# Signed branch outputs and adding DMAs for the right operand of two projection phases

## The chip, the cores and the metric

The kernel runs on one core of a Trainium2 chip. The metric is the device time of one execution in microseconds (us), shown as the median of several runs. The core has a matrix engine (PE), a vector engine (DVE), an activation engine (ACT), a general engine (POOL, GpSimd) and a queue engine (SP). They run beside each other and meet at semaphores. DMA transfers are issued from the queues of SP, ACT and POOL and are carried by sixteen DMA engines. In this kernel only transfers issued on POOL's queue add to what lies at their target; those of SP and ACT copy.

## The reference

The reference is one layer of an encoder: a stream of 1024 positions of width 1024 (16 learned meta tokens stand ahead of it inside), a retention branch and a windowed attention branch, and a merge of both.

```python
u = _rms_norm(h, pre_w)
z = u @ w_in
rq, rk, rv, rg, aq, ak, av, ag, gr, ga = _split_in(z)
...                                              # o_r: retention, normed per head; o_a: attention
o_r = o_r * ret_nw * silu(rg);   y_r = o_r @ w_rb
o_a = o_a * silu(ag);            y_a = o_a @ w_ab
mix = sigmoid(gr) * y_r + sigmoid(ga) * y_a
return h + _rms_norm(mix @ w_o, post_w)
```

All is float32. The change concerns the operands of `o_r @ w_rb` and `o_a @ w_ab`: two products of 1024 by 1024 matrices.

## The kernel before, in words

**Precision.** A float32 product is made of three matmuls of rounded parts: high times high, low times high, high times low (`mm3`, lines 74 to 79). So every operand is split first: ACT writes the rounded high part (a copy with a cast), DVE the low part, which is the source less the high part (`dve_lo`, line 92).

**Order of the work.** First come the projections for retention with retention itself (to about 330 us), then attention with its projections (to about 555 us), and then four phases that are run by one routine (`run`, line 1191): z (the gates, sixteen units of 256 output channels), r (the product with w_rb, four units), a (the product with w_ab, four units) and o (the output projection). Retention writes its transposed, normed and weighted result to the DRAM tensor `oTr_d` (`finish`, lines 591 to 604: two transposes on PE, two ACT copies with the scale of one column of `rnw`, a DMA per two chunks). Attention writes to `oTa_d` (`stage3`, line 1487: an ACT copy out of PSUM). In phase z the first eight units multiply these two tensors in place by the SiLU of their gates (`z_post`, line 1236).

**The four phases.** Each product is made by the Winograd form of Strassen's scheme: seven block products in place of eight. The left operand is the weights, in blocks A11 to A22 of a unit (128 channels by 512). The right operand is the stream in four blocks of 512 by 512, B11 to B22; the first index is the half of the contraction, the second the half of the positions. The table `PROD` (line 929) names the products:

```python
PROD = {1: ("A11", "B11"), 2: ("A12", "B21"), 3: ("S4", "B22"), 4: ("A22", "T4"), 5: ("S1", "T1"),
        6: ("S2", "T2"), 7: ("S3", "T3")}
```

Here S1 = A21 + A22, S2 = S1 - A11, S3 = A11 - A21, S4 = A12 - S2, and T1 = B12 - B11, T2 = B22 - T1, T3 = B22 - B12, T4 = B21 - T2. The S are made by DVE in `Phase.prepare` (line 978) and split by `Phase.split` (line 972), which is called up to LEAD = 6 products ahead of its use. `Phase.product` (line 1019) issues a product's 12 `mm3` matmuls, and `Phase.combine` (line 1055) empties PSUM: ACT copies some accumulators, DVE adds others, and the `post` routine of the phase follows. Per pair of units the order of products is 1, 5, 6, 2, 7, 3, 4, each for both units in turn.

**The right operand of the next phase** is made while the last fourteen products of a phase run. `refill` (line 1141) gives a table of hooks, counted back from the end of the phase: `load` brings a block in four tiles of 128 by 512 from DRAM (on SP's queue, `act_src`, line 1221), `t1`, `t2`, `t3` and `b21` subtract tiles on DVE (`minus`, line 1152), and `plain` or `split_b` (line 948) splits a tile into its place, where the phase before has read its operand for the last time. There is one refill in phase z (the operand of r, out of `oTr_d`, tiles named z) and one in phase r (the operand of a, out of `oTa_d`, tiles named r). The refill in phase a, for the output weights, has another path: its T blocks were computed earlier and are loaded. The tiles of blocks (0,0) and (1,0) come from a pool with seven places, those of (0,1) and (1,1) from one with eight; a load waits until a place is free.

**What sets the order.** The program is written in the order of the products and hooks. A planner (the tile framework) then simulates the program with its own costs and fixes each engine's order of instructions, taking what is ready in its simulation with the earliest place in the program. On the chip each engine works its list strictly in order: an instruction that waits holds up all behind it on that engine. In retention and attention many places are pinned by hand (`follow`, `issue_after`); in the four phases few are.

**POOL** has no compute in the four phases but one power per row of the output. Its queue carries adding DMAs in phase a (`y_post`, line 1287, into `mx_d`) and in phase o (`o_out`, line 1345, into the output).

The names in the profile follow the tiles: bz, br, ba and bo are the PSUM banks of the phases; lhz, llz, lhr, llr and so on the high and low parts of the left operand; big and T the places of the right operand (T2 to T4 share the name T).

Of the kernel before, what the change touches and what calls it, by code (L numbers as in the profile page):

```python
# [7 lines left out]
F32 = mybir.dt.float32  # L8
R = mybir.dt.float32r
AF = mybir.ActivationFunctionType  # L10
ALU = mybir.AluOpType
# [5 lines left out]
P = 128  # L17
KT = D // P
# [15 lines left out]

def cols(c):
    return (0, NM) if c == 0 else (NM + P * (c - 1), NM + P * c)


@with_exitstack
def block_kernel(ctx: ExitStack, tc: tile.TileContext, x0, xT, x, meta, w_in, w_rb, w_ab, w_out, post_w,  # L40
                 rope, tab, out):
    nc = tc.nc
    PSUM = bass.MemoryType.PSUM

    keep = ctx.enter_context(tc.tile_pool(name="keep", bufs=1))
# [45 lines left out]
    def dve_lo(o, i, hi):  # L91
        return nc.vector.tensor_tensor(o, i, hi.bitcast(F32), ALU.subtract).ins  # L92


    vec = keep.tile([P, 2 * KT], F32, name="vec")
# [1 line left out]
    dtab = keep.tile([P, 28], F32, name="dtab")  # L97
    rcol = keep.tile([P, 9], F32, name="rcol")
    rbc = keep.tile([P, T], F32, name="rbc")
    rnw = keep.tile([P, KT], F32, name="rnw")  # L100
    mhalf = keep.tile([P, 40], F32, name="mhalf")
    nc.vector.memset(mhalf, -0.5)

    def fetch_w(src, u):
# [161 lines left out]
    with tc.tile_pool(name="setup", bufs=1, reuse_waits="tile") as st:  # L266
# [61 lines left out]
        for k in range(KT):  # L328
            t = xr[k]
# [19 lines left out]
        decay_columns()  # L349
        with follow(low):  # L350
            nc.vector.tensor_scalar(nsink, head[:, 29:37], -1.0, None, op0=ALU.mult)
            nc.vector.tensor_copy(rnw, vec[:, KT:2 * KT])
            done = pack_meta()
        split, wv0 = halves_w(U_V)
        raw = fetch_w(w_in, U_V)
# [4 lines left out]
        for c in range(9):  # L360
            a, b = cols(c)
            t = st.tile([P, D if c < 7 else T], F32, tag="xn" if c < 7 else "xr", bufs=7 if c < 7 else KT - 1,
                        name=f"xn{c}")[:, 0:D]
# [94 lines left out]
    def retention(h, fill, begin=lambda: None):  # L458
# [132 lines left out]
        def finish(c):  # L591
            o = op[c - 1]
            to = p1(f"to{h}_{c}")
            for e_ in range(2):
                latest[:] = [nc.tensor.transpose(to[:, P * e_:P * e_ + P], o[:, P * e_:P * e_ + P], ident).ins]
            if c % 2 == 0:
                ost[0] = rp.tile([P, 2, 256], F32, tag="ost", bufs=2, name=f"ost{h}_{c}")
            w0 = P * ((c - 1) % 2)
            for e_ in range(2):
                nc.scalar.activation(ost[0][:, e_, w0:w0 + P], to[:, P * e_:P * e_ + P], AF.Copy,  # L600
                                     scale=rnw[:, 2 * h + e_:2 * h + e_ + 1])
            if c % 2 == 1:
                nc.sync.dma_start(
                    oTr_d[2 * h:2 * h + 2, :, P * (c - 1):P * (c + 1)].rearrange("e p t -> p e t"), ost[0])
# [343 lines left out]
    def split_b(n, k, src):  # L948
        (h, as_), (l, _) = (right(n, s, k) for s in range(2))
        nc.scalar.copy(h, as_(src))  # L950
        dve_lo(l, as_(src), h)

    class Phase:
        def __init__(self, nm, seq, load, post, fetch=None, apart=(), early=(), pre={}):
            self.nm, self.load, self.post, self.fetch, self.pre = nm, load, post, fetch, pre
            self.seq = [(u, p) for u, p in seq if p not in pre.get(u, ())]
            self.apart, self.early = apart, early
            self.raw, self.s, self.ops, self.u, self.e = {}, {}, {}, {}, {}
            self.cur = None

# [10 lines left out]

        def split(self, u, p, src):
            h, l = (lp.tile([P, 4, P], R, tag=t, bufs=LEAD, name=f"{t}{self.nm}{u}_{p}") for t in ("lh", "ll"))
            nc.scalar.copy(h, src)  # L974
            dve_lo(l, src, h)
            self.ops[u, p] = h, l

        def prepare(self, u, p):
            if self.cur is not None and u // 2 != self.cur:
                self.raw = {}  # L980
            self.cur = u // 2
            g = nc.vector.tensor_tensor
            made = {1: 2, 6: 3}.get(p)
            if made not in self.pre.get(u, ()):
                made = None
            for q in (p, made):
                if self.fetch and q in POST and u not in self.early:
                    self.fetch(u, *POST[q])
            if made:
                self.e[u, made] = gtile(f"e{u}{made}")  # L990
                nc.sync.dma_start(self.e[u, made], e_d[u, made])
            if p in (1, 2, 4):
                self.split(u, p, self.block(u, PROD[p][0]))
            elif p == 7:
                t = lp.tile([P, 4, P], F32, tag="st", bufs=3, name=f"st{self.nm}{u}S3")
                g(t, self.block(u, "A11"), self.block(u, "A21"), sub)
                self.split(u, 7, t)
            elif p == 5:
                t = self.s[u] = lp.tile([P, 4, P], F32, tag="st", bufs=3, name=f"st{self.nm}{u}S")
                g(t, self.block(u, "A21"), self.block(u, "A22"), add)  # L1000
                self.split(u, 5, t)
                g(t, t, self.block(u, "A11"), sub)
            elif p == 6:
                t = self.s[u]
                self.split(u, 6, t)
                if u in self.early or 3 in self.pre.get(u, ()):
                    del self.s[u]
                else:
                    g(t, self.block(u, "A12"), t, sub)
            elif u in self.early:  # L1010
                t = lp.tile([P, 4, P], F32, tag="st", bufs=3, name=f"st{self.nm}{u}S4")
                g(t, self.block(u, "A21"), self.block(u, "A22"), add)
                g(t, t, self.block(u, "A11"), sub)
                g(t, self.block(u, "A12"), t, sub)
                self.split(u, 3, t)
            else:
                self.split(u, 3, self.s.pop(u))
# [123 lines left out]
    def refill(nm, src):  # L1141

        x = {}

        def load(i, j):
            def f():
                for k in range(4):
                    x[i, j, k] = t = stage(f"{nm}{i}{j}{k}", j)
                    src(t, 4 * i + k, j)
            return f  # L1150

        def minus(o, a, b):
            nc.vector.tensor_tensor(x[*o], x[*a], x[*b], sub)

        def plain(n, i, j):
            def f():
                for k in range(4):
                    split_b(n, k, x[i, j, k])
            return f

        def t1():
            for k in range(4):
                minus((0, 0, k), (0, 1, k), (0, 0, k))
                split_b("T1", k, x[0, 0, k])

        def t2():
            for k in range(4):
                minus((0, 0, k), (1, 1, k), (0, 0, k))
                split_b("T2", k, x[0, 0, k])

        def t3():
            for k in range(4):
                minus((0, 1, k), (1, 1, k), (0, 1, k))

        def b21():
            for k in range(4):
                split_b("B21", k, x[1, 0, k])
                minus((0, 0, k), (1, 0, k), (0, 0, k))

        def got(n):  # L1180
            return lambda: get_pre(n)

        if nm == "a":
            return {-16: [load(0, 0)], -14: [load(1, 1)], -13: [plain("B11", 0, 0)], -11: [got("T1")],
                    -10: [load(1, 0)], -9: [got("T2")], -7: [plain("B21", 1, 0)], -5: [got("T3")],
                    -3: [plain("B22", 1, 1)], -1: [got("T4")]}
        return {-16: [load(0, 0), load(0, 1)], -14: [load(1, 1)], -13: [plain("B11", 0, 0)], -11: [t1],
                -10: [load(1, 0)], -9: [t2, t3], -7: [b21], -5: [plain("T3", 0, 1)], -3: [plain("B22", 1, 1)],
                -1: [plain("T4", 0, 0)]}

    def run(phases):

# [26 lines left out]
        return load  # L1219

    def act_src(d):
        def src(o, k, j):
            nc.sync.dma_start(o, d[k, :, 512 * j:512 * j + 512])
        return src


# [152 lines left out]
    def attention():  # L1379
# [96 lines left out]
        def stage3(hp, n):  # L1476
            g = hp // 2
            bl, m = st2.pop((hp, n))
            po = p3(f"po{hp}_{n}")
            for j, (b, h_, l_) in enumerate(bl):  # L1480
                mm3(po[:, 0:256], *(t[:, P * g:P * g + P] for t in (vah[:, b], low_value(b))), h_, l_, j == 0, False)
            latest[:] = [nc.tensor.matmul(po[:, 0:256], vm[:, P * g:P * g + P], m, start=False,
                                          stop=True).ins]
            if n % 2 == 0:
                oa[0] = ap.tile([P, 2, 256], F32, tag="oa", bufs=2, name=f"oa{hp}_{n}")
            o0 = P * (n % 2)
            last["oa"] = nc.scalar.copy(oa[0][:, :, o0:o0 + P],
                                        po[:, 0:256].rearrange("p (e t) -> p e t", e=2)).ins
            if n % 2:
                nc.scalar.dma_start(  # L1490
                    oTa_d[2 * hp:2 * hp + 2, :, P * (n - 1):P * (n + 1)].rearrange("e p t -> p e t"), oa[0])
# [181 lines left out]
```

## Time and profile before

| what | value |
|---|---|
| median of 3 runs | 1047.88 us (1046.16 to 1048.37) |
| the profiled execution | 1045.47 us |
| its span, first to last instruction | 1043.4 us |
| granted TensorE clock, mean | 0.998 |
| bytes moved by DMA | 188.43 MB, 181 GB/s over the span |
| phase z ends, phase r starts | about 796 to 808 us |
| phase r ends, phase a starts | about 874 to 885 us |
| first and last matmul of phase o | 951.8 and 1036.1 us |

The page gives, for each engine, the busy time, its share of the span and the count of instructions. The list of waits tells which engine stood idle at which line, and whose instruction released it. The time line shows single instructions with their start and duration, with the idle time before them in brackets. A table by windows gives the busy time of all engines in a stretch of the span. For a DMA, the time to landing runs from its issue to the completion of its last byte. Busy spans of matmuls overlap a little, since they are pipelined: two starts lie closer than one duration.

### The profile page before, as it was taken

To read this page: it belongs to the slowest core of one execution; us is meant where nothing else is said; L and a number is where in the kernel's file an instruction comes from. 1 tells how busy PE (TensorE), PEld (TensorE's weight loads), DVE (VectorE), ACT (ScalarE), POOL (GpSimd) and SP (SyncE) were. 2 spreads that over 40 slices of the span, in tenths; PEclk is the share of its full clock that TensorE was granted. 3 is DMA by queue.
4 is the path that set the end of the run, shared out by engine and by line. 5 is a ranking of instruction groups with operands and counts; after the bars stand their busy time and mean duration, and the time that the engine had idled before them with its cause. 6 is when DMAs were issued, how large, how long until landed. Compare 5 with 4: busy or idle time off the path is not lost. (4 is left out here: it accounts for less than half of the span.)

```text
span 1043.4 us, 17240 instructions
## 1 busy us (share of the span) xinstructions
PE 1029.0 (99%) x5880; PEld 901.9 (86%) x5880; DVE 838.1 (80%) x1788; ACT 505.7 (48%) x1127; POOL 228.2 (22%) x338
## 2 busy tenths in 40 slices
PE   9999999999999999999999999999999999999997
PEld 8998999989989888988888888777888788788886
DVE  7786758768875787878769988998899899778665
ACT  5541432423524566665677554555557446334443
POOL 3444244243342333443310000000000000111042
PEclk9999999999999999999999999999999999999999
DMA  9434223243231466676549679899935746799563
GB/s 353 165 88 88 64 46 85 78 88 103 78 91 62 102 182 188 172 184 164 162 165 340 191 255 322 308 325 346 392 109 178 248 159 231 223 236 317 134 122 80
DMA packets 98838, 188.43 MB, mean 181 GB/s; under 512 B 13024, under 2 KB 37632, under 8 KB 98192
## 3 DMA queue, kind: packets, MB, share of 16 engines
q1 hardware_dynamic: 81200, 162.89, 46.5%
q0 software_dynamic: 10176, 14.73, 9.4%
q10 hardware_dynamic: 7376, 9.73, 2.7%
q8 instruction: 46, 0.75, 0.3%
q14 instruction: 40, 0.33, 0.1%
HBM read 124.32 MB, written 57.68 MB: 174 GB/s over the span
## 5 line engine op out<-in xcount | busy, mean ns | idle before, releaser
L1287 POOL DMA_DIRECT2D mx_d<-c1a x4 | 3.6, 889 | 395.7 <-DVE c1a L1278 377.5
L77 PE MATMUL bz<-big,llz 128*128 128x512 f32 x192 | 74.9, 390 | 0.2 <-DVE llz L92 0.2
L76 PE MATMUL bz<-big,lhz 128*128 128x512 f32 x192 | 74.0, 390 | 0.5 <-ACT lhz L974 0.5
L78 PE MATMUL bz<-big,lhz 128*128 128x512 f32 x192 | 74.2, 389 | 0.0
L76 PE MATMUL pv<-wh,big 128*128 128x256 f32 x256 | 72.8, 284 | 0.0
L77 PE MATMUL pv<-wh,big 128*128 128x256 f32 x256 | 72.7, 284 | 0.0
L78 PE MATMUL pv<-wl,big 128*128 128x256 f32 x256 | 72.7, 284 | 0.0
L77 PE MATMUL bz<-T,llz 128*128 128x512 f32 x176 | 68.6, 390 | 0.7 <-DVE llz L92 0.7
L76 PE MATMUL bz<-T,lhz 128*128 128x512 f32 x176 | 68.2, 390 | 0.5 <-DVE u2z L1064 0.5
L78 PE MATMUL bz<-T,lhz 128*128 128x512 f32 x176 | 68.5, 389 | 0.0
L1419 ACT ACTIVATE p<-raw,nm 128x401 f32<-128x401 f32 (+1 forms) x64 | 38.3, 600 | 34.7 <-DVE nm L1416 33.3
L1429 POOL TENSOR_SCALAR p<-p,den 128x400 f32<-128x400 f32 (+1 forms) x60 | 37.8, 687 | 67.1 <-DVE den L1422 65.2
L76 PE MATMUL paq<-big,wh 128*128 128x512 f32 x128 | 51.5, 402 | 0.0
L77 PE MATMUL paq<-big,wl 128*128 128x512 f32 x128 | 50.2, 392 | 0.1
L78 PE MATMUL paq<-big,wh 128*128 128x512 f32 x128 | 50.2, 393 | 0.0
L76 PEld LDWEIGHTS pv<-wh,big 128*128 128x128 f32 x256 | 48.3, 189 | 0.4
L77 PEld LDWEIGHTS pv<-wh,big 128*128 128x128 f32 x256 | 48.3, 189 | 0.4
L78 PEld LDWEIGHTS pv<-wl,big 128*128 128x128 f32 x256 | 48.2, 188 | 0.3
L76 PEld LDWEIGHTS bz<-big,lhz 128*128 128x128 f32 x192 | 36.1, 188 | 8.5 <-ACT lhz L974 1.1
L92 DVE TENSOR_TENSOR wl<-wr,wh 128x1024 fp32r<-128x1024 f32 x28 | 35.1, 1258 | 10.0 <-POOL wh L89 6.7
L77 PEld LDWEIGHTS bz<-big,llz 128*128 128x128 f32 x192 | 36.0, 188 | 7.9 <-DVE llz L92 0.5
L78 PEld LDWEIGHTS bz<-big,lhz 128*128 128x128 f32 x192 | 36.0, 188 | 7.5
(616 smaller groups left out, 3594.7 us busy)
## 6 DMA issues: line engine op xcount, KB each, us to landing
wrz<-in_w_in_dram SPq DMA_DIRECT2D x32, 512.0 KB, 6.1
wr<-in_w_in_dram SPq DMA_DIRECT2D x29, 512.0 KB, 4.0
we<-in_w_in_dram SPq DMA_DIRECT2D x16, 512.0 KB, 4.2
tg<-tg_d SPq DMA_DIRECT2D x32, 256.0 KB, 4.9
e<-e ACTq DMA_DIRECT2D x20, 256.0 KB, 2.6
e<-e SPq DMA_DIRECT2D x20, 256.0 KB, 4.9
xn<-in_x_dram SPq DMA_DIRECT2D x8, 512.0 KB, 9.6
oTr_d<-ost SPq DMA_DIRECT2D x16, 256.0 KB, 2.1
```

The lines of the kernel that those rows point to most:

```text
L76: nc.tensor.matmul(o, ah, bh, start=first, stop=False, **kw)
L77: nc.tensor.matmul(o, al, bh, start=False, stop=False, **kw)
L78: latest[:] = [nc.tensor.matmul(o, ah, bl, start=False, stop=last, **kw).ins]
L92: return nc.vector.tensor_tensor(o, i, hi.bitcast(F32), ALU.subtract).ins
L1287: nc.gpsimd.dma_start(d, to, accum_op=ALU.add)
L1419: last["exp"] = nc.scalar.activation(p[:, 0:1 + wid], raw[e_][:, 0:1 + wid], AF.Exp, scale=-1.0, bias=nm_[:, e_:e_ + 1], accum_out=den[:, ...
L1429: nc.gpsimd.tensor_scalar(pt[e_][:, 0:wid], pt[e_][:, 0:wid], den[:, e_:e_ + 1], 1.0, op0=ALU.mult, op1=ALU.mult)
```

## The change

Half of the branch outputs are stored with the opposite sign, namely blocks B11 and B22 of both right operands. `turned_sign` says which: heads in the first half of the channels with positions in the first half, and second half with second half. For retention the sign comes from a second set of columns in `rnw`, for attention from the scale of the copy out of PSUM. The gating multiplies, so the sign stays.

The differences are then sums, and the DMA queue of GpSimd adds them in place. B12 is added to the tile that holds -B11, which gives T1. Adding -B22 gives -T2, and adding B21 gives T4 as the kernel uses it. A tile with B12, to which -B22 is added, gives -T3. Each sum is split before the next is added to the same tile. `t1`, `t2`, `t3`, `b21` and `minus` are gone. The left operands of the products with a turned right operand are turned too, in the phases r and a only: products 1 and 3 in the split, S2 and S3 by exchanged operands of the subtraction, S4 by an addition. The table `rnw` grows by eight columns and `mhalf` shrinks by eight.

```diff
+def turned_sign(h, c):
+    return h // 2 == c // 4
...
-            nc.vector.tensor_copy(rnw, vec[:, KT:2 * KT])
+            nc.vector.tensor_copy(rnw[:, 0:KT], vec[:, KT:2 * KT])
+            nc.vector.tensor_scalar(rnw[:, KT:2 * KT], vec[:, KT:2 * KT], -1.0, None, op0=ALU.mult)
...
+            s0 = 2 * h + (KT if turned_sign(h, c - 1) else 0)
...
-                                     scale=rnw[:, 2 * h + e_:2 * h + e_ + 1])
+                                     scale=rnw[:, s0 + e_:s0 + e_ + 1])
...
-            nc.scalar.copy(h, src)
-            dve_lo(l, src, h)
+            if self.turned and p in (1, 3):
+                nc.scalar.activation(h, src, AF.Copy, scale=-1.0)
+                nc.vector.scalar_tensor_tensor(l, src, -1.0, h.bitcast(F32), op0=mul, op1=sub)
+            else:
+                nc.scalar.copy(h, src)
+                dve_lo(l, src, h)
...
-                g(t, self.block(u, "A11"), self.block(u, "A21"), sub)
+                g(t, self.block(u, "A21" if self.turned else "A11"), self.block(u, "A11" if self.turned else "A21"), sub)
...
-                g(t, t, self.block(u, "A11"), sub)
+                if self.turned:
+                    g(t, self.block(u, "A11"), t, sub)
+                else:
+                    g(t, t, self.block(u, "A11"), sub)
...
-                    g(t, self.block(u, "A12"), t, sub)
+                    g(t, self.block(u, "A12"), t, add if self.turned else sub)
...
-        def minus(o, a, b):
-            nc.vector.tensor_tensor(x[*o], x[*a], x[*b], sub)
+        def grow(o, a):
+            def f():
+                for k in range(4):
+                    src(x[*o, k], 4 * a[0] + k, a[1], True)
+            return f
...
-        return {-16: [load(0, 0), load(0, 1)], -14: [load(1, 1)], -13: [plain("B11", 0, 0)], -11: [t1],
-                -10: [load(1, 0)], -9: [t2, t3], -7: [b21], -5: [plain("T3", 0, 1)], -3: [plain("B22", 1, 1)],
-                -1: [plain("T4", 0, 0)]}
+        return {-16: [load(0, 0), load(0, 1)], -14: [load(1, 1)], -13: [plain("B11", 0, 0), grow((0, 0), (0, 1))],
+                -12: [grow((0, 1), (1, 1))], -11: [plain("T1", 0, 0), grow((0, 0), (1, 1))], -10: [load(1, 0)],
+                -9: [plain("T2", 0, 0), grow((0, 0), (1, 0))], -7: [plain("B21", 1, 0)], -5: [plain("T3", 0, 1)],
+                -3: [plain("B22", 1, 1)], -1: [plain("T4", 0, 0)]}
...
-        def src(o, k, j):
-            nc.sync.dma_start(o, d[k, :, 512 * j:512 * j + 512])
+        def src(o, k, j, more=False):
+            s = d[k, :, 512 * j:512 * j + 512]
+            if more:
+                nc.gpsimd.dma_start(o, s, accum_op=ALU.add)
+            else:
+                nc.sync.dma_start(o, s)
...
-            last["oa"] = nc.scalar.copy(oa[0][:, :, o0:o0 + P],
-                                        po[:, 0:256].rearrange("p (e t) -> p e t", e=2)).ins
+            last["oa"] = nc.scalar.activation(oa[0][:, :, o0:o0 + P],
+                                              po[:, 0:256].rearrange("p (e t) -> p e t", e=2), AF.Copy,
+                                              scale=-1.0 if turned_sign(hp, n) else 1.0).ins
```

More of the change, by code (lines that the diff above doesn't have):

```diff
@@ L99, in block_kernel @@
     rbc = keep.tile([P, T], F32, name="rbc")
-    rnw = keep.tile([P, KT], F32, name="rnw")
-    mhalf = keep.tile([P, 40], F32, name="mhalf")
+    rnw = keep.tile([P, 2 * KT], F32, name="rnw")
+    mhalf = keep.tile([P, 32], F32, name="mhalf")
     nc.vector.memset(mhalf, -0.5)
@@ L956, in __init__ @@
             self.seq = [(u, p) for u, p in seq if p not in pre.get(u, ())]
-            self.apart, self.early = apart, early
+            self.apart, self.early, self.turned = apart, early, nm in ("r", "a")
             self.raw, self.s, self.ops, self.u, self.e = {}, {}, {}, {}, {}
```

15 lines of the change are left out of this document (removed).

## The prediction

> **What bounds the kernel now.** I read the page's busy times first, then the list of waits of PE, then the time line of PE where those waits lie.
>
> ```profile
> span 1043.4 us, 17240 instructions
> PE 1029.0 (99%) x5880; PEld 901.9 (86%) x5880; DVE 838.1 (80%) x1788; ACT 505.7 (48%) x1127; POOL 228.2 (22%) x338
> ```
>
> PE is busy 1029.0 of 1043.4 us, so it bounds the kernel, and 14.4 us is all that it stands still. The change removes no matmul. Work taken from DVE is worth only what PE waits for it, and that is in the list of PE's waits (who waited for whom: total, times, longest):
>
> ```profile
> PE idle L313 <- DVE warm L207: 1.4, 1, 1.4
> PE pq L76 <- ACT big L333: 1.1, 1, 1.1
> PE bz L77 <- DVE llz L92: 0.9, 2, 0.7
> PE ba L77 <- DVE lla L92: 0.9, 1, 0.9
> PE br L77 <- DVE llr L92: 0.8, 2, 0.6
> PE bz L76 <- ACT lhz L974: 0.5, 1, 0.5
> PE bz L76 <- DVE u2z L1064: 0.5, 1, 0.5
> ```
>
> The first two are the start. The three with bz are the z phase before the change acts (its longest, 0.7, is at 723). What the change can reach is br and ba, the two phases whose right operand it makes another way. The time line of PE shows where (start, duration, idle before in brackets):
>
> ```profile
> 813.49 0.50 PE L77 MATMUL br<-big,llr 128*128 128x512 f32 x1 [0.24 <-DVE llr L92]
> 817.10 0.50 PE L77 MATMUL br<-T,llr 128*128 128x512 f32 x1 [0.57 <-DVE llr L92]
> 891.74 0.50 PE L77 MATMUL ba<-big,lla 128*128 128x512 f32 x1 [0.89 <-DVE lla L92]
> ```
>
> All three come just after DVE has made a new right operand. I call the two stretches windows 1 and 2 (columns: length, busy us and count of PE, PEld, DVE, ACT, POOL; granted clock; DMA share; GB/s):
>
> ```profile
> 763.90:829.00 65.10, 64.29 (x282) 52.58 (x281) 61.48 (x102) 41.22 (x75) 0.00 (x0) 1.00 0.50 166
> 847.00:905.00 58.00, 57.11 (x251) 46.66 (x250) 54.81 (x91) 32.96 (x59) 0.00 (x0) 1.00 0.55 187
> ```
>
> DVE works 61.5 of 65.1 and 54.8 of 58.0 us: it is the late one there. ACT has 24 and 25 us free, POOL does nothing.
>
> **The change, part by part.** *The differences leave DVE.* The prices of what goes and of what is replaced:
>
> ```profile
> L1153 DVE TENSOR_TENSOR z<-z,z x16: 679/681/683, 771.2 to 801.9; 128x512 f32<-128x512 f32 x16
> L1153 DVE TENSOR_TENSOR r<-r,r x16: 679/681/684, 850.1 to 879.0; 128x512 f32<-128x512 f32 x16
> L92 DVE TENSOR_TENSOR llr<-wrr,lhr 128x512 fp32r<-128x512 f32 x12 | 8.1, 684 | 1.0 <-ACT lhr L974 1.0
> L1278 DVE SCALAR_TENSOR_TENSOR c1r<-tg,c1r 128x512 f32<-128x512 f32 x4 | 2.7, 682 | 0.0
> L974 ACT CAST lhr<-wrr 128x512 fp32r<-128x512 f32 x12 | 7.4, 621 | 1.4 <-PE br L78 1.3
> L1243 ACT ACTIVATE c1z<-c1z 128x512 f32<-128x512 f32 x8 | 5.1, 632 | 4.0 <-DVE c1z L1239 4.0
> L1487 ACT COPY oa<-po 128x256 f32<-128x256 f32 x32 | 11.9, 373 | 26.4 <-PE po L1482 25.7 <-PE ps L78 0.4
> L532 ACT ACTIVATE op<-pa,rcol 128x256 f32<-128x256 f32 x32 | 15.2, 476 | 48.9 <-PE pa L78 48.4
> L352 DVE COPY rnw<-vec x1: 157/157/157, 22.8 to 22.8; 128x8 f32<-128x8 f32 x1
> ```
>
> 16 subtractions of 681 ns leave each window: 10.9 us of DVE where it lacked 0.81 and 0.89 us. That is more than enough to end the three stalls: between 0 (the order of the engines keeps another instruction late) and 0.24 + 0.57 + 0.89 = 1.70 us. I take -1.7. Next late are ACT's casts, below.
>
> *The signs.* Per phase eight splits (units 0 to 3, products 1 and 3) take a SCALAR_TENSOR_TENSOR for a TENSOR_TENSOR (682 against 684 ns: nothing) and an ACTIVATE for a CAST (632 against 621: 0.1 us in eight, on an ACT with 24 us free). S2, S3 and S4 have their operands turned, at no cost. The copy of attention's output becomes an ACTIVATE: by the row of L532, which also reads a scale per partition, at most 32 x 0.103 = 3.3 us of ACT; that stage's ACT waits 25.7 us for these very products (L1487), so I take 0. The column of signs adds one DVE instruction like L352, 0.16 us, at 23 us, where no PE wait on DVE is listed: 0.
>
> *The adding DMAs.* 16 of 256 KB per refill, which nothing replaces: the 16 plain loads stay. The nearest rows are the adding DMAs that POOL issues already (issues: count, KB, us to landing; then the window of the busiest burst, eight of them, and the line of its issues in the list of one tile):
>
> ```profile
> mx_d<-c5a POOLq DMA_DIRECT2D x4, 256.0 KB, 7.5
> out_dram<-c1o POOLq DMA_DIRECT2D x3, 256.0 KB, 4.0
> aq<-m_aq POOLq DMA_DIRECT2D x32, 128.0 KB, 4.0
> akr<-m_ak POOLq DMA_DIRECT2D x12, 64.0 KB, 3.7
> 994.00:1006.00 12.00, 12.00 (x55) 9.93 (x54) 11.38 (x21) 4.65 (x11) 9.33 (x11) 1.00 0.88 123
> L1345 POOL DMA_DIRECT2D out_dram<-c5o x3: 986/1122/1223, 995.2 to 1028.5; - x3
> q0 software_dynamic: 10176, 14.73, 9.4%
> ```
>
> On POOL one issue costs 0.9 to 1.2 us, 16 some 18 us of an engine with nothing else in either window; the queue's next own work, the adding into mx_d, comes later. As load: the queue of the page's part 3 holds 9.4% of 1043.4 us for 14.73 MB, 1.75 us of all sixteen engines per 256 KB; the burst gives 0.88 x 12 / 8 = 1.3. So 21 to 28 us a refill. Window 1 has 65.1 x 0.50 = 32 us free, window 2 has 58 x 0.45 = 26: full at the upper end.
>
> *Are the operands in time?* Each block is now a chain: split, add, split, add. The rows for it (time line of DVE, the fourth and last split of B11; then the reads of T2 to T4, which share the name T, T2 first):
>
> ```profile
> 774.85 0.68 DVE L92 TENSOR_TENSOR big<-z,big 128x512 fp32r<-128x512 f32 x1
> L76 PE MATMUL br<-T,lhr x44: 387/389/397, 816.1 to 876.0; 128*128 128x512 f32 x44
> 851.90 0.68 DVE L92 TENSOR_TENSOR big<-r,big 128x512 fp32r<-128x512 f32 x1
> L76 PE MATMUL ba<-T,lha x44: 388/389/398, 894.4 to 958.8; 128*128 128x512 f32 x44
> ```
>
> With 0.9 us to issue, 7.5 to land and 1.3 (0.62 + 0.68) to split, a link is 9.7 us. From 775.5: T1 is there at 785, T2 at 795, T4 at 805. A product is 12 matmuls of 64.29/282 us, 2.7 us. T2 is first read at 816.1, T1 two products earlier, 810.7, T4 eight later, 838. The reserve is 21 us and more; in phase a T2 is there at 872 for 894.4. T3 needs one link. PE waits for no operand itself: 0. That cover is gone when a link lasts twice as long, 20 us. SP's queue: its loads of the next operand wait for these buffers. x10's come free sooner (no subtraction reads them), x00's after T4's split, 805 and 882 by the chain; now the subtractions run to 801.9 and 879.0 and the last splits follow them. So SP stands no longer than now: 0.
>
> *The new wait.* What can hurt is the queue of ACT. Its casts of T1, T2 and T4 stand in an order that the planner fixed by its own idea of a DMA; if the sum lands later, ACT stands still. Behind it are the casts of the left operand (lhr, lha) and the copies that empty PSUM (c1, u2, u3); DVE's low halves wait for the casts, PE for both. T3 is added early, so three groups a refill, six in all. The nearest rows are ACT's waits for the adding DMAs of attention and for plain loads:
>
> ```profile
> ACT kTh L713 <- DMA akr<-m_ak: 6.3, 5, 2.3
> ACT aqh L667 <- DMA aq<-m_aq: 5.6, 3, 2.4
> ACT wh L118 <- DMA wr<-in_w_in_dram: 6.7, 3, 4.5
> ACT lhz L974 <- DMA wrz<-in_w_in_dram: 6.3, 3, 2.7
> ```
>
> The first two: eight waits, 11.9 us, 1.5 each, for transfers of 3.7 to 4.0 us. At 7.5 us to landing I estimate 3 us a group, 18 us of ACT in all, within what it has free. How much reaches PE? The four rows are 24.9 us of ACT, and PE's waits that could go back to them are 0.5 (lhz) and 0.9 (llz): at most 6%. So 18 us give up to 1.0; I take 0.7. The ends are 0 and, if a group stands still for all of its 7.5 us while PE has some 3 us of work in hand (estimate), 6 x 4.5 = 27. I stay near the low end because it is the nearer row: the same engine behind the same kind of DMA.
>
> **Sum.** -1.7 + 0.7 = -1.0 us. The profiled execution took 1045.47 us (span 1043.4 and 2.07 around it): 1044.5 after. It stands 2.4 us under the median of the runs, 1047.88; with the same distance the median becomes 1046.9.
>
> **A rule that speaks against the change.** In the burst above DVE worked 11.38 of 12 us, and POOL's issues still took 0.9 to 1.2 us. The Trainium skill, page "SBUF — State Buffer", section "SBUF: two separate sides", warns of a trap: DMAs from GpSimd's queue have descriptors that GpSimd writes itself, and VectorE in a two-port mode locks it out of the port. A later section of that page, "Who interferes with whom", says that tensor_tensor has no such mode, and most of DVE's work in both windows is TENSOR_TENSOR. The trace agrees as far as it goes: no row names a mode.
>
> **The rivals.**
> *Slower, by ACT's queue.* A sum lands late, ACT stands before T1 or T2 at the head of phases r and a, where PE had no work in hand at 813, 817 and 891, and the wait passes to PE. For it: the landings reach 7.5 us, four follow each other at 1.3 to 1.75 us, and the planner chose the order blind to that. Against it: 6% in the rows above, and DVE is no longer behind. It decides once PE loses more than 1.7 + 2.1 = 3.8 us in six groups. At 1.3 us a group (4.5 us of wait less 3.2 in hand) it is 6 x 1.3 - 1.7 = +6: 1054. With half of that, +2.2: 1050.
> *Slower, by full DMA engines in window 2.* At 28 us against 26 free the weights for phase a come late. For it: its share is 0.55 now, and the same loads are waited for already:
>
> ```profile
> DVE sta3S L1000 <- DMA wra<-in_w_ab_dram: 2.5, 1, 2.5
> ```
>
> Against: PE does not feel those 2.5 us now. Doubled and passed on, +5 - 1.7: 1051.
> *Slower, by order.* The planner sees other costs for attention's copies and orders another stage anew, with stalls like the 0.5 to 0.9 us above, five of them: +3.5 - 1.0: 1050.4.
> *Slower, by a locked port.* If DVE's stream held up POOL's descriptors, each of 32 issues would wait for the DVE instruction ahead of it, 0.7 us: 22 us, and with half of it passed on, +11 - 1.7: 1057. The page's trap is this mechanism; the burst's issues speak against it.
> *Faster.* All of 1.7 us goes, nothing comes, and the new order also drops the 1.9 us of bz: 1047.9 - 3.6 = 1044.3. It needs luck: the bz stalls lie ahead of both windows, where only the order could move them.
>
> **Chances.** About 0.2% (2.1 us) is what a measurement of this kernel can tell from no change. Forecast, within 0.2%: 0.46. Faster by more: 0.18. Slower: 0.36, of it ACT's queue 0.18, DMA engines 0.08, order 0.08, port 0.02. The terms alone give 1046.2 (no new wait) to 1050 (half the queue's price). The range goes from 1044.6, close to the faster end, to 1053.0, which leaves out the port and the worse half of the queue.
>
> **What would show it.** Right: no subtraction rows of z and r on DVE, 32 more issues on POOL at 0.9 to 1.2 us, DVE near 51 and 44 us busy in the two windows, no wait of br and ba on llr and lla, ACT's big and T casts waiting for DMA some 3 us a group, PE still at 1029 us. Wrong: PE waits on lhr, lha or on copies from PSUM around 780 to 905; landings of the sums over 9 us; weights wrr or wra waited for; new PE waits in attention.

## The result, and the profile after

The changed kernel takes 1060.38 us (median of 4 runs, 1059.58 to 1061.06) beside 1048.00 for the kernel before on the same chip: a ratio of 1.0129, 95% interval 1.0110 to 1.0148. The forecast was 1046.9 with a range to 1053.0; it was wrong, and on the slow side. The profiled execution has a span of 1059.2 us, 15.8 more than before.

The page of the changed kernel (span; busy time of each engine):

```profile
span 1059.2 us, 17303 instructions
PE 1033.7 (98%) x5880; PEld 906.5 (86%) x5880; DVE 821.6 (78%) x1757; ACT 506.5 (48%) x1127; POOL 254.8 (24%) x370
```

PE stands still for 1059.2 - 1033.7 = 25.5 us, before for 14.4: 11.1 us more. Its busy time grew by 4.7 us with the same 5880 matmuls, so it also ran slower somewhere. DVE lost 16.5 us of work; the 32 subtractions that went are 21.8 us at 681 ns each, and the difference was not followed up. The time line of PE tells where the idle time is:

```profile
801.04 0.80 PE L81 MATMUL bz<-T,lhz 128*128 128x512 f32 x1 [7.82 <-ACT u3z L1075]
888.69 0.80 PE L81 MATMUL br<-big,lhr 128*128 128x512 f32 x1 [5.52 <-DVE u3r L1078]
```

The three stalls of before (br and ba on llr and lla, 1.7 us) are gone from the list of PE's waits. In their place stand two long ones, one per refill, both on a PSUM bank that ACT or DVE had not yet emptied. 7.8 + 5.5 - 1.7 = 11.6 us, which is the added idle time but for half a microsecond.

What held ACT and DVE up? The time lines of ACT and DVE just ahead of the two stalls, and the two loads that ACT waited for, as SP issued them:

```profile
799.88 0.62 ACT L957 CAST big<-z 128x512 fp32r<-128x512 f32 x1 [5.72 <-DMA z<-oTr_d]
800.40 0.58 ACT L1075 COPY u3z<-bz 128x512 f32<-128x512 f32 x1
888.56 0.62 ACT L957 CAST big<-r 128x512 fp32r<-128x512 f32 x1 [7.16 <-DMA r<-oTa_d]
```

```profile
886.74 0.69 DVE L1011 TENSOR_TENSOR sta0S<-wra,wra 128x512 f32<-128x512 f32 x1 [4.37 <-DMA wra<-in_w_ab_dram]
887.95 0.68 DVE L1078 TENSOR_TENSOR u3r<-u3r,br 128x512 f32<-128x512 f32 x1
```

```profile
793.62 0.33 SPq L1226 DMA_DIRECT2D z<-oTr_d  x1
880.34 0.57 SPq L1226 DMA_DIRECT2D r<-oTa_d  x1
```

The casts at 799.88 and 888.56 read the fourth tile of B21. That is no sum: it is a plain load on SP's queue. It was issued at 793.62 and 880.34, so it was 6.3 and 8.2 us on its way. Behind the first of these casts stands the copy u3z that PE needs, 0.5 us later. In the second refill DVE stands for the weights wra, also a plain load, and u3r, which PE needs, is two instructions behind. In the kernel before, the same cast came 2.9 us after the issue of its load, in the second refill too (time lines of SP and ACT in the first):

```profile
793.05 0.33 SPq L1223 DMA_DIRECT2D z<-oTr_d  x1
```

```profile
794.39 0.58 ACT L1061 COPY u3z<-bz 128x512 f32<-128x512 f32 x1
795.92 0.61 ACT L950 CAST big<-z 128x512 fp32r<-128x512 f32 x1
```

The order changed as well. In the kernel before, both copies u3z of this refill (791.30 and 794.39) stand ahead of the cast on ACT, and DVE's first addition to u3z (795.92) stands ahead of str0S (798.92), the first sum of weights for phase r, made out of wrr. In the changed kernel the cast is ahead of both copies, and str0S ahead of the addition.

Why do plain loads land late? The table by windows, for the stretches in which twelve of each refill's sixteen adds are issued, first the kernel before, then the changed one (the last two columns are the DMA share and GB/s):

```profile
772.00:800.00 28.00, 28.00 (x126) 23.17 (x125) 28.00 (x47) 20.44 (x38) 0.00 (x0) 1.00 0.32 97
858.00:882.00 24.00, 24.00 (x107) 19.87 (x107) 24.00 (x42) 15.36 (x28) 0.00 (x0) 1.00 0.56 186
```

```profile
772.00:800.00 28.00, 21.22 (x94) 17.25 (x92) 17.09 (x28) 13.29 (x25) 10.46 (x12) 0.92 0.95 183
858.00:882.00 24.00, 23.95 (x106) 19.49 (x105) 15.47 (x25) 14.26 (x27) 10.51 (x12) 1.00 0.86 151
```

The engines are nearly full there (0.95 and 0.86), at only 183 and 151 GB/s. The queue rows and issue rows of the changed kernel (to landing in us, last number):

```profile
q0 software_dynamic: 14784, 23.12, 14.2%
```

```profile
z<-oTr_d POOLq DMA_DIRECT2D x16, 256.0 KB, 6.7
r<-oTa_d POOLq DMA_DIRECT2D x16, 256.0 KB, 6.3
wrr<-in_w_rb_dram SPq DMA_DIRECT2D x8, 512.0 KB, 6.1
wra<-in_w_ab_dram SPq DMA_DIRECT2D x8, 512.0 KB, 6.0
```

```profile
wrr<-in_w_rb_dram SPq DMA_DIRECT2D x8, 512.0 KB, 3.9
wra<-in_w_ab_dram SPq DMA_DIRECT2D x8, 512.0 KB, 4.3
```

The second fence is the kernel before: the weights' landing grew by about 2 us. POOL's queue held 9.4% of 1043.4 = 98.1 us before and 14.2% of 1059.2 = 150.4 us now: 52.3 us for 32 adds, **1.63 us of all sixteen engines for each 256 KB**. Twelve adds are 19.6 us. Before, the stretches of 28 and 24 us had 28 x 0.68 = 19.0 and 24 x 0.44 = 10.6 us free.

Last, the slower matmuls. The table by windows right after each stall (the clock is the third number from the end):

```profile
801.00:803.00 2.00, 1.96 (x5) 1.60 (x6) 2.00 (x5) 2.00 (x5) 0.00 (x0) 0.50 0.92 333
888.70:890.70 2.00, 2.00 (x5) 1.63 (x6) 2.00 (x4) 2.00 (x5) 0.00 (x0) 0.50 0.86 301
894.70:896.70 2.00, 2.00 (x10) 1.60 (x10) 2.00 (x4) 1.30 (x3) 0.00 (x0) 0.99 0.87 332
```

For 4 to 6 us after each stall PE is granted half its clock and starts 5 to 7 matmuls in 2 us, where it starts 9 or 10 otherwise. In steps of 2 us from 801 to 807 and from 888.7 to 894.7 it starts 37. At the 9 per step of the kernel before (126 in 28 us) these would be 54: 17 too few, at 0.22 us each about 3.8 us, most of the 4.7 us of busy time.

### The profile page after: what moved, and what is told of

Read it like the earlier page. It is cut to its first block, busy times and chain, and to the rows that moved or that the text cites. A ratio compares the mean times of both kernels' runs of the same rounds, so it can differ in the third digit from the quotient of the medians.

```text
span 1059.2 us, 17303 instructions
## 1 busy us (share of the span) xinstructions
PE 1033.7 (98%) x5880; PEld 906.5 (86%) x5880; DVE 821.6 (78%) x1757; ACT 506.5 (48%) x1127; POOL 254.8 (24%) x370
## 3 DMA queue, kind: packets, MB, share of 16 engines
q0 software_dynamic: 14784, 23.12, 14.2%
## 5 line engine op out<-in xcount | busy, mean ns | idle before, releaser
L1224 POOL DMA_DIRECT2D z<-oTr_d x16 | 14.1, 983 | 246.5 <-DMA wrz<-in_w_in_dram 200.8
L81 PEld LDWEIGHTS bz<-T,lhz 128*128 128x128 f32 x176 | 33.4, 190 | 16.7 <-ACT u3z L1075 8.2
```

Of the source, the lines that this page charges most:

```text
L81: nc.tensor.matmul(o, ah, bh, start=first, stop=False, **kw)
L1224: nc.gpsimd.dma_start(o, s, accum_op=ALU.add)
```

## The experiments

The theory after this reading: **the adding fills the sixteen engines, so plain loads that are issued beside it land late, and ACT and DVE, which work in a fixed order, stand for them with PE's copies behind.** Its rivals: the order alone (one cast in an unlucky place), the signs and the changed left operand, and the chain of waits for the sums.

### The parts alone: no adding; signs alone

No adding: the 32 transfers on POOL's queue stay, but copy and don't add. The sums are left out, so the right operands are not those of the reference.

```diff
-                nc.gpsimd.dma_start(o, s, accum_op=ALU.add)
+                nc.gpsimd.dma_start(o, s)
```

> The changed kernel with the same transfers on POOL's queue as plain copies: nothing is added, so the right operands are wrong blocks (the sums are left out); the order on all engines is the same. Theory full DMA engines (an adding transfer costs 1.6 us of all sixteen engines, a plain one 0.8): the plain load of the fourth tile lands in 3 to 4 us in place of 6.3 and 8.2, PE's two waits shrink to under 2 us each; about 1048 us. Rival chain (the time lies in the dependent links, split, transfer, split, whatever the transfer does): landings of 5 us stay, PE still waits over 8 us; 1055 to 1060 us.

Measured: 1043.22 us, ratio 0.9974 (0.9960 to 0.9988). The page, POOL's queue and its rows:

```profile
PE 1027.1 (99%) x5880; PEld 902.5 (87%) x5880; DVE 821.4 (79%) x1757; ACT 506.4 (49%) x1127; POOL 245.0 (24%) x370
q0 software_dynamic: 12736, 23.12, 12.0%
```

```profile
z<-oTr_d POOLq DMA_DIRECT2D x16, 256.0 KB, 3.9
```

The same bytes, 23.12 MB, with ACT, DVE and POOL in the same order at the two refills: (0.120 x 1039.8 - 98.1) / 32 = 0.83 us of the engines per transfer, half of what an add takes, and 3.9 us to landing in place of 6.7. The two long stalls are gone (the longest on u3z is 0.8 us) and the kernel is faster than before, by more than the first theory said (1048). The fourth tile's cast comes 4.3 and 5.2 us after the issue of its load, in place of 6.3 and 8.2; 3 to 4 were expected. Idle time of PE: 1039.8 - 1027.1 = 12.7, that is 1.7 us less than before.

Signs alone: everything of the change but the adding DMAs; sixteen DVE additions per refill make the sums.

```diff
-                    src(x[*o, k], 4 * a[0] + k, a[1], True)
+                    nc.vector.tensor_tensor(x[*o, k], x[*o, k], x[*a, k], add)
```

> The changed kernel with the signs, but the sums made by 16 additions on DVE per refill, out of the loaded tiles, in place of the adding DMAs. If all of the loss is the adding DMAs and what they do to the order: as before, 1046 to 1050 us, PE's waits of br and ba back at some 1.7 us. If the signs (ACTIVATE for COPY and CAST, turned operands) cost anything: over 1050 us, with new waits of PE in attention or in the two phases.

Measured: 1045.30 us, ratio 0.9994 (0.9982 to 1.0006). The three stalls of 0.24, 0.59 and 0.89 us are back. So the signs and the left operands cost nothing that shows, and the loss comes with the adding. ACT and DVE here take the casts of the late tile, the copies u3 and the new weights in the order of the kernel before, so this run doesn't part the adding from the order; the run above does.

### The order: the fourth tile's cast moved behind the copy

```diff
-                -9: [...], -7: [plain("B21", 1, 0)], -5: [plain("T3", 0, 1)],
+                -9: [...], -7: [plain("B21", 1, 0, range(3))],
+                -5: [plain("T3", 0, 1)], -4: [plain("B21", 1, 0, (3,), True)],
```

Here the last argument pins the fourth tile's split, in the planner's order, behind the latest copy out of PSUM.

> The changed kernel, but the cast of the fourth tile of B21 (and its low half) stands on ACT behind the copies u3 that empty PSUM, in both refills; all else keeps its place. Theory order (ACT stands 5.7 and 7.2 us for that one plain load, and the copies behind it hold PE): both waits of PE, 7.8 and 5.5 us, go, with the halved clock behind them; 1045 to 1049 us. Rival late sums (ACT is late from each sum in turn, and through it the weights of the next phase come late): the first wait shrinks to 2 to 4 us, the second stays at 3 us or more; 1051 to 1056 us.

Measured: 1058.66 us, ratio 1.0123 (1.0101 to 1.0145): almost nothing was gained, and the time lies above both forecasts. PE's waits and the time line of DVE:

```profile
PE br L81 <- DVE u3r L1078: 4.9, 1, 4.9
PE bz L81 <- DVE u3z L1078: 4.5, 1, 4.5
```

```profile
802.56 0.69 DVE L1011 TENSOR_TENSOR str0S<-wrr,wrr 128x512 f32<-128x512 f32 x1 [4.50 <-DMA wrr<-in_w_rb_dram]
```

With the cast out of the way, the next plain load takes its place: DVE stands for wrr, with u3z behind it. In this order the place of the one cast decides only which late load is felt. DVE's str0S kept its place ahead of the addition to u3z here.

### One refill alone

The refill in phase z adds by DMA, the one in phase r by DVE (a condition on the phase's name in `grow`).

> The refill in phase z as in the change (sixteen adding DMAs), the refill in phase r by sixteen DVE additions. If each refill makes its own stall: PE waits 6 to 9 us near 801, none above 2 us near 888, half the clock for 4 to 6 us after the first only, time 1053 to 1056. If the second stall is a consequence of the first (things shifted by it), it is there too or both go: 1058 to 1061, or 1046.

Measured: 1054.10 us, ratio 1.0079 (1.0061 to 1.0097). PE's waits and the cast:

```profile
PE bz L81 <- ACT u3z L1075: 8.9, 1, 8.9
```

```profile
801.01 0.62 ACT L957 CAST big<-z 128x512 fp32r<-128x512 f32 x1 [6.55 <-DMA z<-oTr_d]
```

As forecast for stalls of their own: one stall, half the clock for some 6 us behind it, none above 1 us in the second refill, and 0.8 of the 1.3%.

### How much adding is too much

`grow` adds some groups by DMA and the others by DVE: only T3 (four adds per refill), T3 and T4 (eight), or all but T2 (twelve). A fourth kernel keeps all sixteen adds and their chain, and adds half the columns of each tile, so that the other half of the sums is left out. The first diff shows the kernel with T3; the conditions of the next two name T3 and T4, and all but T2. The second diff is the fourth kernel.

```diff
+                    if o == (0, 1):
                         src(x[*o, k], 4 * a[0] + k, a[1], True)
+                    else:
+                        nc.vector.tensor_tensor(x[*o, k], x[*o, k], x[*a, k], add)
```

```diff
-                nc.gpsimd.dma_start(o, s, accum_op=ALU.add)
+                nc.gpsimd.dma_start(o[:, 0:256], s[:, 0:256], accum_op=ALU.add)
```

> Only T3 is made by adding DMAs (four per refill, issued early and needed late); the sums for T1, T2 and T4 are made by twelve DVE additions per refill. If the engine time of the adding is the cause and matters only once the sixteen engines are full, eight adds (13 us of all engines by 1.63 each) fit into what the windows leave: no PE wait above 2 us, the plain loads of B21's fourth tile and of wrr and wra land in 4 to 6 us, time 1043.5 to 1046.5. If each add costs its share whatever the load (14.3 us by 32 adds), it is 8 x 0.45 = 3.6 us slower than before: about 1049.5.

> T3 and the last step to T4 by adding DMAs (eight per refill), T1 and T2 by DVE additions. If fullness decides: DMA share of the windows around 0.85 to 0.9, PE waits at the two places of the changed kernel gone or below 2 us, time 1044 to 1049. If each add costs its share: half the loss, about 1053.

> Twelve adding DMAs per refill: T1, T3 and T4 as in the change, the step to T2 by DVE additions. Eight per refill gave 1041.6, sixteen 1060.4. If a threshold of load decides (12 x 1.63 = 20 us a refill against 26 to 32 free): between 1042 and 1050, with one late load at most, in the second refill. If the loss grows evenly from eight on: about 1051. If the chain of the group T2 alone makes the stalls: 1042.

> All sixteen adding DMAs per refill, but each adds only the first 256 of the 512 columns of its tile (128 KB); the sums of the other columns are left out. The chain split, add, split, add, its waits and its order stay, the engine time of the adding halves to about 13 us a refill. If the load decides: as with eight whole adds, no PE wait above 2 us, 1041 to 1045. If the chain decides, since a transfer of 128 KB still takes 4 us or more to land: PE waits of 3 us and more at the two places, 1050 to 1058.

| adds per refill | engine time of the adding, 1.63 us each | us | ratio (95%) |
|---|---|---|---|
| none, DVE adds | 0 | 1045.30 | 0.9994 (0.9982 to 1.0006) |
| 4: T3 | 6.5 | 1041.99 | 0.9965 (0.9953 to 0.9977) |
| 8: T3, T4 | 13 | 1041.63 | 0.9973 (0.9962 to 0.9984) |
| 16 of half the size | 15 (0.92 us each, from its queue's share) | 1044.35 | 0.9988 (0.9975 to 1.0001) |
| 12: all but T2 | 20 | 1052.74 | 1.0071 (1.0054 to 1.0088) |
| 16: the change | 26 | 1060.38 | 1.0129 (1.0110 to 1.0148) |

Up to some 15 us per refill the adding costs nothing or less; between 15 and 20 the loss sets in. Four and eight adds came out better than either theory had said, twelve as bad as an even loss from eight on would make it, and the half-size kernel within the forecast of the load. It has the whole chain of splits and sums, and its longest stall is 1.8 us. So the chain by itself isn't what loses the time. Two of these kernels beat both the kernel before and the change.

The rows differ in more than the amount, since the planner orders each kernel anew. The one with half-size adds has the order of the change at both places. With eight adds the fourth tile's cast comes as late after its issue as in the change, 7.9 and 7.6 us (issued at 787.32 and 863.53), but it was issued earlier, ACT stands for it only 2.2 and 2.5 us, and in the first refill a copy u3z runs ahead of it:

```profile
789.82 0.59 ACT L1075 COPY u3z<-bz 128x512 f32<-128x512 f32 x1 [2.04 <-PE bz L83]
795.19 0.62 ACT L957 CAST big<-z 128x512 fp32r<-128x512 f32 x1 [2.19 <-DMA z<-oTr_d]
```

PE's longest wait at the two places is 0.3 us. So a late load alone isn't the loss; it costs time where PE's next copy or addition stands behind its reader.

Below stand the page with T3 alone, where PE's longest wait in the four phases is 0.5 us, and then PE's and DVE's waits with twelve adds:

```profile
span 1040.9 us, 17278 instructions
PE 1028.1 (99%) x5880; PEld 902.3 (87%) x5880; DVE 832.1 (80%) x1781; ACT 506.2 (49%) x1127; POOL 234.8 (23%) x346
```

```profile
PE bz L81 <- DVE u3z L1078: 4.5, 1, 4.5
PE br L81 <- DVE u3r L1078: 3.5, 1, 3.5
DVE sta0S L1011 <- DMA wra<-in_w_ab_dram: 5.2, 1, 5.2
DVE str0S L1011 <- DMA wrr<-in_w_rb_dram: 4.6, 1, 4.6
```

### The load alone, with nobody waiting for it

All sums by DVE; beside them sixteen adding DMAs per refill from DRAM into a scratch in DRAM that nobody reads. In a first version POOL copies one column of the sum's tile ahead of each, but the planner set the transfers before those copies.

```diff
+                    nc.vector.tensor_tensor(x[*o, k], x[*o, k], x[*a, k], add)
+                    nc.gpsimd.tensor_copy(pace, x[*o, k][:, 0:1])
+                    src(scr_d[k], 4 * a[0] + k, a[1], True)
```

> All sums by DVE additions, and beside them sixteen adding DMAs of 256 KB per refill, at the same places of the order, from DRAM into a scratch in DRAM that nobody reads: the load of the adding without anything that waits for a sum. If the load alone delays the plain loads (B21's fourth tile, wrr, wra land over 5.5 us) and so PE: PE waits of 3 to 8 us near 801 and 888, 1052 to 1060. If the chain split, add, split, add is what loses the time: no PE wait above 2 us, 1044 to 1049.

Measured: 1074.02 us, ratio 1.0268 (1.0249 to 1.0287). The adds ran between 590 and 735 us, in phase z, not where they were meant to; neither expectation can be judged by it. PE's longest stall, 11.6 us, comes at their end, behind a plain load that DVE waits for (time line of DVE):

```profile
734.37 0.69 DVE L782 TENSOR_TENSOR w<-w,w 128x512 f32<-128x512 f32 x1 [11.03 <-DMA w<-in_w_out_dram]
```

These loads take 7.4 us to land (median), with the sums by DVE alone 5.8. They were also issued later, the last at 726.1 where it was 703.5, so not all of the 11 us is landing. In the second version each transfer is pinned behind its copy.

```diff
-                    nc.gpsimd.tensor_copy(pace, x[*o, k][:, 0:1])
-                    src(scr_d[k], 4 * a[0] + k, a[1], True)
+                    with follow(nc.gpsimd.tensor_copy(pace, x[*o, k][:, 0:1]).ins):
+                        src(scr_d[k], 4 * a[0] + k, a[1], True)
```

> As the earlier kernel with unread adding DMAs from DRAM into a scratch in DRAM, but on POOL's queue each of them now stands behind a copy of one column that POOL takes from the tile whose sum DVE has just made; so the adds run between about 772 and 810 and between 850 and 885 and not in phase z. All sums are made by DVE and PE's order is that of the kernel with signs and DVE sums (1045.3, span 1043.2). If the load on the sixteen engines is enough: DMA share near 1 in the stretches, wrr, wra and B21's fourth tile land over 5.5 us, PE waits of 3 us or more on what they feed, 1050 to 1060. If a chain of waits for sums is needed as well: PE's waits stay at the three stalls of 0.24 to 0.9 us and the time within 1044 to 1048.

Measured: 1052.26 us, ratio 1.0055 (1.0035 to 1.0076). The time line of ACT and PE's longest wait:

```profile
793.17 0.58 ACT L1076 COPY u3z<-bz 128x512 f32<-128x512 f32 x1
799.94 0.62 ACT L958 CAST big<-z 128x512 fp32r<-128x512 f32 x1 [5.13 <-DMA z<-oTr_d]
881.65 0.62 ACT L958 CAST big<-r 128x512 fp32r<-128x512 f32 x1 [4.85 <-DMA r<-oTa_d]
```

```profile
PE ba L82 <- DVE lla L97: 3.5, 1, 3.5
```

The fourth tile of B21 is late again, by 5.1 and 4.9 us of ACT and 7.1 and 6.9 us after its issue, though neither ACT, DVE nor PE waits for any of these adds. The load alone makes the late loads. The time falls into the forecast of the load, 1050 to 1060, near its lower end.

PE's stalls are smaller than in the change and stand at other places (1.6 and 1.4 us beside the 3.5). The order tells why the two long ones are missing: ACT's is that of the kernel with sums by DVE, and its last copy u3z runs at 793.17, ahead of the cast. With a tile about as late, the kernel in this order loses 0.55%, the change 1.29%. The two differ in more than the order (nobody waits for these adds), so the share of the order alone stays open. Why the smaller stalls stand just there was followed up no further.

### What stands ahead of the loads

In the changed kernel the four adds for T4 are issued at 787.0 to 791.6, right ahead of the loads that land late. Here POOL lets them wait until the fourth tile of B21 has landed, by copying a column of it first; then the same with the sum for T2 by DVE as well.

```diff
+                late = follow(nc.gpsimd.tensor_copy(pace, x[1, 0, 3][:, 0:1]).ins) if (o, a) == ((0, 0), (1, 0)) else ExitStack()
+                with late:
                   for k in range(4):
                       src(x[*o, k], 4 * a[0] + k, a[1], True)
```

> The change with one edit: the four adds for T4 of each refill wait on POOL for the fourth tile of B21 to have landed (POOL copies one column of it first). In the changed kernel these four are issued at 787.0 to 791.6, right ahead of the loads of wrr (about 792) and of that tile (793.6), which land 6 to 8 us after their issue. Sixteen adds per refill stay, and the engines' orders stay but for a handful of rows. If what counts is the adding that stands ahead of a plain load in the sixteen engines (four adds are 4 x 1.63 = 6.5 us): that tile and wrr land in 3 to 5 us, ACT's wait for it falls from 5.7 to below 3 us, PE's 7.8 us near 801 to below 4 and with it most of the half clock: 1045 to 1053. If the sum of the adding in the stretch counts, or the waits for the sums of T1 and T2: PE's stalls stay at 6 to 8 us, 1057 to 1062.

> Both edits at once: the step to T2 by DVE additions (twelve adding DMAs per refill) and the four adds for T4 behind the landing of B21's fourth tile. Alone they gave ratios of 1.0071 and 1.0076 against 1.0129 for the change, so they took 0.6 and 0.5 per cent. If the waits for the sums of T2 and the adding ahead of the plain loads are two separate costs, they add up: a ratio near 1.002, about 1048, PE's two stalls of 4.5 and 3.5 us (with T2 by DVE) fall below 2 us each. If both edits take the same thing away, it stays near 1.007, 1053.

Measured: 1053.21 us, ratio 1.0076 (1.0053 to 1.0098), and 1047.60 us, ratio 1.0026 (1.0013 to 1.0039). PE's and ACT's waits of the first kernel:

```profile
PE bz L81 <- ACT u3z L1076: 6.0, 1, 6.0
ACT big L958 <- DMA z<-oTr_d: 9.8, 4, 3.8
```

The four adds ahead of the loads are worth 0.5%, the four adds for T2 and ACT's waits for their sums 0.6%, and both together 1.0%: two costs that nearly add up, as the second expectation said (a ratio near 1.002; the first stall is gone, the second is 2.3 us and not below 2). The 0.6% holds a change of order too: with T2 by DVE one copy u3z stands ahead of the cast again. Of the first expectation the landing came true: the fourth tile's cast comes 4.3 and 4.8 us after the issue of its load. The time was just missed (1053.2 against 1053), and so were the waits: the tile's wait fell from 5.7 to 3.8 us, not below 3, and the first stall only to 6.0 us, where ACT had also stood 9.8 - 3.8 = 6.0 us for three sums. So the waits for sums seem to matter once the engines are full; with half-size adds they did not. Over all these kernels the fourth tile's time from issue to cast goes with what stands right ahead of its load, not with the number of adds: 7.9 and 7.6 us with eight adds a refill, T4's four just ahead, and 4.3 and 4.8 us with sixteen, T4's behind. What a single add does to a single load can't be told from these runs.

## Why the prediction was wrong

**The differences leave DVE, -1.7 us: right.** The three stalls went. The term itself can be read where the long stalls are missing: the idle time of PE fell by 1.7 us without the adding and by 14.4 - 12.8 = 1.6 with T3 alone. The medians fell somewhat more, 0.26 and 0.35%; the rest is in PE's busy time and no row explains it. DVE's busy time in the two windows was forecast near 51 and 44 us and is 49.8 and 43.0, though the stalls shift some work out of these windows.

**The signs, 0: right** (0.9994). **The order: half seen.** The rival expected small new stalls in another stage, and those did not come. The order alone loses nothing: with plain copies it gave 0.9974. But the planner did put readers of the late loads ahead of u3z, and so PE stood when these loads came late.

**The price of an add: right.** 21 to 28 us per refill were forecast; 16 x 1.63 is 26. POOL's issues take 0.87 and 0.88 us (medians), forecast 0.9 to 1.2, and no row shows them held up by a running DVE instruction: nothing of the locked port shows. Landing takes 6.3 to 6.7 us, below the 7.5 assumed.

**The room for them: here the working failed first.** 26 us were set against the free time of whole windows, 32 and 26 us in 65 and 58. But twelve of the sixteen are issued within 21 us. In the stretches of 28 and 24 us around them 19.0 and 10.6 us were free for 19.6. The profile before held these numbers; the windows were cut too wide.

**"SP stands no longer than now: 0": true of the issue in the first refill, and beside the point.** SP issued the fourth tile at 793.62, before at 793.05. What was not costed is the time from there to landing, 6.3 and 8.2 us against at most 2.9.

**The new wait on ACT's queue, +0.7: the term that broke the sum.** ACT's time standing for the sums was put at 18 us. Its waits for the tiles of z and r are 28.3 us in four rows:

```profile
ACT big L957 <- DMA z<-oTr_d: 11.7, 4, 5.7
ACT big L957 <- DMA r<-oTa_d: 10.1, 5, 7.2
ACT T L957 <- DMA r<-oTa_d: 4.9, 3, 3.8
ACT T L957 <- DMA z<-oTr_d: 1.6, 2, 0.9
```

The longest of the first two rows, 5.7 and 7.2, are the plain loads of the fourth tile, 12.9 us that no term held. The other 15.4 us are the sums, not far from the 18. So the waits for sums were well sized, the plain loads were put at nothing, and what reaches PE was wrong: put at 6%, from stages whose ACT waits had PE work in hand. Here PE lost 13.3 us, partly by DVE's own late load: about half as much as ACT stood. An average over other stages said nothing about a cast with PE's next PSUM copy directly behind it. ACT's time line before showed how near they are: the copy u3z at 794.39, the cast at 795.92, close enough to change places.

The reading of PE's waits had also set bz aside as "the z phase before the change acts". The first refill runs inside that phase, and the longest stall stands on a bz bank, at 801.

**The half clock** was in no term, some 4 us. Two of the rivals each held a half of the truth: ACT's queue (1054, 0.18) with waits but for sums, and full DMA engines with weights that come late in window 2 (1051, 0.08). They were priced as alternatives, and they were one mechanism in both windows; its 1060 lay outside the range and below the end of 27 us that the working itself had named.

## What to carry to other kernels

A transfer's room is to be counted in the stretch in which its burst is issued, not in the whole stage: here 12 adds in 21 us. A burst on POOL's queue delayed the plain loads of SP's here; look for the loads issued just behind the burst, and for what stands behind their readers on engines that work in order. In this kernel it paid to move to the DMA queue only what is early and needed late: T3 alone, four adds of sixteen, kept the gain (0.9965), and all of them turned it into a loss (1.0129).

## What the runs showed of the hardware

An adding transfer of 256 KB from DRAM took 1.63 us of all sixteen engines, the plain one of the same size on the same queue 0.83, both worked out from the share that POOL's queue holds.

After a long enough idle time PE's granted clock drops to half. A stall of 1.76 us (half-size kernel) left it at 1.00; one of 1.94 us (sixteen adds, T4 behind) brought a stretch of half clock, as these rows of their time lines and tables by windows show:

```profile
798.50 0.50 PE L81 MATMUL bz<-T,lhz 128*128 128x512 f32 x1 [1.76 <-ACT u3z L1075]
```

```profile
798.50:800.50 2.00, 2.00 (x9) 1.66 (x10) 2.00 (x5) 2.00 (x5) 0.00 (x0) 1.00 0.75 282
```

```profile
882.25 0.59 PE L81 MATMUL br<-big,lhr 128*128 128x512 f32 x1 [1.94 <-DVE u3r L1079]
```

```profile
883.00:885.00 2.00, 2.00 (x6) 1.54 (x5) 2.00 (x4) 2.00 (x5) 2.00 (x4) 0.50 1.03 403
```

The Trainium skill, page "TensorE: Matmul & The Clock Gate", section "HAM oscillation — how this bites in real kernels", gives the rule "no PE-idle gaps >~3.4µs". The traces agree in kind, but here 1.94 us was enough. So PE's stalls aren't all worth their own length: the 13.3 us of the change cost some 4 us more, the stalls of under 1 us in the kernel before none that shows.
